# MLP of a decode-step layer: sums of the second projection's right factors stored beside the first projection's outputs, tiles over both token parts, and one sequence of products for both projections

## The chip, the core and the metric

One core of a Trainium2 chip runs the whole program. The engines named below are TensorE (PE; its weight loads are PEld), VectorE (DVE), ScalarE (ACT), GpSimd (POOL) and SyncE (SP), whose queue issues nearly all of the DMAs here. The metric is the device time of one execution in microseconds, the median of the runs shown.

## The reference

One layer of a hybrid network is computed for 1024 prompt tokens and 8 sample tokens of 1024 features, all in float32: three attention-like branches, their gated sum, an output projection, and an MLP. The change concerns the MLP alone:

```
x  = x + merged @ w_out
h2 = rmsnorm(x, norm_ffn)
x  = x + square(relu(h2 @ w_up)) @ w_down        # w_up 1024 x 4096, w_down 4096 x 1024
```

## The kernel before

Activations lie feature-major, 128 features on the partitions and 1032 tokens in a row. A float32 product is made of three: each factor is split into a high half, which the matrix engine takes exactly (a copy on ACT), and a low half (a subtraction on DVE, in the helper `low`, line 1310), and high x high, high x low and low x high are added up in PSUM.

From the output projection on, the tokens are taken in four quarters of 258 (`HQ`). Quarter l x part s: the part s (0 or 1) pairs two quarters, l (0 or 1) is the half of tokens in Strassen's scheme. Both projections of the MLP use Winograd's form of that scheme: 7 products P1 to P7 instead of 8, whose **left factors** are blocks of weights or sums of them (S1 to S4), and whose **right factors** are blocks of activations or sums of them (T1 = B12 - B11, T2 = B22 - T1, T3 = B22 - B12, T4 = B21 - T2). `CHAIN` says which PSUM bank a product adds into: P1, P6, P7 and P4 run up in one bank (two such banks), P5 and P3 in another, P2 in a third, and the partial sums are read on the way. So P6 has to wait until P1's sum was read, P7 for P6's, P4 for P7's, and P3 for P5's.

`stream` runs through units of seven products, in the order P1, P5, P4 of the unit before, P6, P2, P3, P7. It makes left factors ahead, as far as there are places for them (six in the first projection, four in the second): the sums on POOL (`add`, line 1460), the high half on ACT (line 1489), the low half on DVE. Weights are loaded two units ahead.

- **First projection** (`w_up`): 16 units of 256 hidden features; a product is 24 matmuls of 258 columns. `done_up` reads the sums out, applies the squared ReLU, and leaves four tiles `us` of 128 x 516 (128 features; l is fixed, both parts s), which SP stores in DRAM as `u`.
- **Second projection** (`w_down`): 24 units. The contraction over 4096 hidden features is cut into six parts of 2, 3, 3, 3, 3, 2 pairs of hidden blocks, and each part has four units j = 0 to 3 of 256 output features; a product is 12 or 18 matmuls. `done_dn` adds each of the seven products to the residual `x` (line 1636, DVE, 128 x 516).
- **Right factors of the second projection.** For each of the 16 pairs r, `feed` loads its four blocks from `u` into tiles `ub`, and makes T1, T2 and T3 on POOL (`sums`, lines 1326 to 1328), T4 later (lines 1588, 1645 or 1669). `factor` splits each of the seven, for each part s by itself: 14 copies on ACT (line 1320) and 14 subtractions on DVE, 128 x 258 each. The first two pairs are fed while the first projection runs; the others while the second one does. In a part, one or two pairs are fed ahead, the rest (`late`) during its last unit j = 3, when the part's own factors come free.

Code is written in this order, but instructions are put on the engines by a list scheduler that moves what it takes to be ready; each engine then works through its own list in order, and an instruction that waits holds up all behind it.

Of the kernel before, what the change touches and what calls it, by code (L numbers as in the profile page):

```python
# [89 lines left out]
def tile_step(ctx, tc, I, O):  # L90
# [98 lines left out]
    # activations in feature-major form, as pairs of exact halves, one tile for each group of tokens  # L189
# [64 lines left out]
    def in_proj(c0, evac):  # L254
        # a piece is split once the products two pieces before it have been taken out, not when it is thought to arrive
# [57 lines left out]
    # the loras' weights as exact halves: the high one over both halves of their inputs, the low one over the high  # L313
# [155 lines left out]
        # k, and for each head the sums that normalize kk and that weigh v beside the state; both go from a column per  # L469
        # head to all of its features by way of DRAM  # L470
# [52 lines left out]
        # scaled by the decay within each chunk  # L523
# [13 lines left out]
        # products within each chunk, and token-major forms  # L537
# [15 lines left out]
        # (the latter as they count at the end of their chunk)  # L553
# [15 lines left out]
        # inverse of the unit lower triangular matrices: first of their two diagonal blocks, each partition  # L569
        # with a quarter of the columns of one block  # L570
# [18 lines left out]
        # and the block beside them, two matrices in a product of which the diagonal blocks count  # L589
# [15 lines left out]
        # chunk after chunk, both pairs at once  # L605
# [41 lines left out]
        # group norm, then the sum and the gate  # L647
# [29 lines left out]
        # a sample's part of the window that stays  # L677
# [59 lines left out]
    # last token's projections  # L737
# [76 lines left out]
    def rwkv_sample():  # L814
        # one step of the sample group, a half of a head's values in each partition
# [64 lines left out]
    def xsample():  # L880
        # the sample group: scores by products along the features, since each sample has its own memory
# [124 lines left out]
    # keys  # L1006
# [24 lines left out]
    # values  # L1031
# [116 lines left out]
    def ssample():  # L1148
        # the sample group: each sample has its own past keys and values
# [87 lines left out]
    def split_out(pool, d, x=""):  # L1237
        # a branch's output, as a pair of exact halves
# [73 lines left out]
    def parts(t):  # L1312
        # a row of tokens in its four quarters
# [4 lines left out]
    def factor(key, s, i, x):  # L1318
        hi, lo = mk(cb[s], f"h{i}", [P, HQ], F32R, 4), mk(cb[s], f"l{i}", [P, HQ], F32R, 4)
        A.activation(hi, x, AF.Copy)  # L1320
        low(lo, x, hi)
        right[key, s, i] = hi, lo

    def sums(b11, b12, b21, b22, t1, t2, eng):
        # T1, T2 and T3; T3 takes the place of B12
# [363 lines left out]
    for r in pairs[0][2:]:  # L1689
        for _ in feeding(r):  # L1690
            pass
# [29 lines left out]
```

## Time and profile before

| | us |
|---|---|
| median of 3 runs | 2095.15 |
| fastest, slowest of the 3 | 2092.27, 2095.73 |
| the profiled execution, from its first to its last instruction (span) | 2090.5 |
| busy in it: PE, DVE, ACT, POOL | 1931.6, 1381.6, 765.4, 569.6 |
| first projection | about 1350 to 1698 |
| second projection | about 1698 to 2081 |

For the profiled execution only the span is given, no time of its own: it is 4.65 us under the median, and this distance is taken to be outside the program's instructions. A time worked out as a change of the span is therefore carried over to the median as it is. PE is busy for 92% of the span. In a program whose stages are all bound by the same engine the remaining 8% would be spread evenly; the table of stretches further down tells whether they are.

### The profile page before, as it was taken

The numbers are of one execution on the slowest core, as the hardware profiler recorded it, in microseconds if no ns is written. First come the engines' busy times: TensorE is split into PE (matmuls) and PEld (weight loads), VectorE is DVE, ScalarE is ACT, GpSimd is POOL, SyncE is SP. The second block draws the span as 40 slices with busy tenths as digits, with TensorE's granted clock in tenths as the row PEclk, the third lists the DMA queues.
The fourth block names the chain that finished last, engine by engine and source line by source line (L and its number), as shares of the span: only waits on it lengthen the run. The fifth ranks groups of instructions, "written<-read, shape, count | busy, mean of one in ns | idle before, by whom it ended". The sixth has DMA issues, their size and how long they took to land. (4 is left out here: it accounts for less than half of the span.)

```text
span 2090.5 us, 36979 instructions
## 1 busy us (share of the span) xinstructions
PE 1931.6 (92%) x14079; PEld 1832.6 (88%) x14079; DVE 1381.6 (66%) x3359; ACT 765.4 (37%) x1729; POOL 569.6 (27%) x606
## 2 busy tenths in 40 slices
PE   4989889999999989999899999889999988998898
PEld 4879878888888978998799999879999988998897
DVE  7455767576765375676723674885545599888974
ACT  5432333232323244345641132443333353433433
POOL 3422111110110244231110000364222246456531
PEclk9999989798989999999899999989999999999999
DMA  4543223323221154232253446334333353222213
GB/s 140 167 161 117 87 73 93 83 85 91 82 78 36 58 187 133 52 116 71 81 168 123 154 131 209 97 96 128 117 97 107 107 198 102 88 83 90 78 45 102
DMA packets 243278, 225.31 MB, mean 108 GB/s; under 512 B 41565, under 2 KB 203422, under 8 KB 243102
## 3 DMA queue, kind: packets, MB, share of 16 engines
q1 hardware_dynamic: 240832, 215.88, 33.5%
q0 software_dynamic: 2016, 6.53, 1.0%
q8 instruction: 111, 1.82, 0.4%
q10 hardware_dynamic: 254, 0.55, 0.1%
q14 instruction: 65, 0.53, 0.1%
HBM read 161.51 MB, written 61.78 MB: 107 GB/s over the span
## 5 line engine op out<-in xcount | busy, mean ns | idle before, releaser
L181 PE MATMUL mm<-hh,wh 128*128 128x384 f32 (+1 forms) x1152 | 391.6, 340 | 5.4 <-ACT z L342 4.8
L182 PE MATMUL mm<-hl,wh 128*128 128x384 f32 (+1 forms) x1152 | 388.9, 338 | 7.3 <-DVE hl L217 7.3
L183 PE MATMUL mm<-hh,wl 128*128 128x384 f32 (+1 forms) x1152 | 388.4, 337 | 1.3 <-POOL wl L174 1.3
L1506 PE MATMUL z<-h,wh 128*128 128x258 f32 x1504 | 269.6, 287 | 22.4 <-DVE x L1636 9.0
L1506 PE MATMUL z<-h,wl 128*128 128x258 f32 x1488 | 265.3, 287 | 22.8 <-DVE x L1636 21.5
L1506 PEld LDWEIGHTS z<-h,wh 128*128 128x128 f32 x1504 | 220.8, 193 | 26.8 <-issue 6.0
L1506 PEld LDWEIGHTS z<-h,wl 128*128 128x128 f32 x1488 | 217.1, 192 | 25.9 <-issue 18.3
L182 PEld LDWEIGHTS mm<-hl,wh 128*128 128x128 f32 x1152 | 227.0, 197 | 11.3 <-DVE hl L217 8.2
L181 PEld LDWEIGHTS mm<-hh,wh 128*128 128x128 f32 x1152 | 227.4, 197 | 9.5 <-ACT z L342 5.2
L183 PEld LDWEIGHTS mm<-hh,wl 128*128 128x128 f32 x1152 | 227.3, 197 | 5.0 <-POOL wl L174 1.7
L174 POOL TENSOR_TENSOR wl<-wst,wh 128x1024 fp32r<-128x1024 f32 x48 | 116.8, 2434 | 213.6 <-ACT wh L173 210.1
L1506 PE MATMUL z<-l,wl 128*128 128x258 f32 x744 | 153.9, 287 | 3.1 <-DVE l L1310 3.1
L1506 PE MATMUL z<-l,wh 128*128 128x258 f32 x752 | 155.8, 287 | 1.0 <-DVE l L1310 1.0
L1636 DVE TENSOR_TENSOR x<-z,x 128x516 f32<-128x516 f32 x168 | 115.4, 687 | 56.3 <-PE z L1506 56.3
L173 ACT ACTIVATE wh<-wst 128x1024 fp32r<-128x1024 f32 x84 | 88.8, 1057 | 138.6 <-PE mm L182 74.1
L1310 DVE TENSOR_TENSOR l<-ub,h 128x258 fp32r<-128x258 f32 x224 | 124.0, 602 | 1.4 <-ACT h L1320 1.3
L1506 PEld LDWEIGHTS z<-l,wh 128*128 128x128 f32 x752 | 119.7, 194 | 1.7 <-DVE l L1310 1.7
L1506 PEld LDWEIGHTS z<-l,wl 128*128 128x128 f32 x744 | 117.8, 192 | 3.7 <-DVE l L1310 3.6
L1320 ACT ACTIVATE h<-ub 128x258 fp32r<-128x258 f32 x224 | 78.6, 409 | 67.3 <-POOL ub L1645 31.4
L183 PE MATMUL mm<-oh,wl 128*128 128x384 f32 (+1 forms) x288 | 92.2, 320 | 0.0
L182 PE MATMUL mm<-ol,wh 128*128 128x384 f32 (+1 forms) x288 | 92.1, 320 | 0.0
L181 PE MATMUL mm<-oh,wh 128*128 128x384 f32 (+1 forms) x288 | 92.0, 319 | 0.0
(518 smaller groups left out, 4247.5 us busy)
## 6 DMA issues: line engine op xcount, KB each, us to landing
wst<-in_w_in SPq DMA_DIRECT2D x48, 512.0 KB
u<-us SPq DMA_DIRECT2D x64, 258.0 KB
ub<-u SPq DMA_DIRECT2D x64, 258.0 KB
wst<-in_w_down SPq DMA_DIRECT2D x24, 512.0 KB
gate<-gt SPq DMA_DIRECT2D x48, 192.0 KB
gl<-gate SPq DMA_DIRECT2D x16, 516.0 KB
wst<-in_w_out SPq DMA_DIRECT2D x16, 512.0 KB
wst<-in_w_up SPq DMA_DIRECT2D x16, 512.0 KB
```

Of the source, the lines that this page charges most:

```text
L173: A.activation(hi, st, AF.Copy)
L174: last_lo[:] = [eng.tensor_tensor(lo, st, hi.bitcast(F32), ALU.subtract)]
L181: PE.matmul(out, lhsT=wh, rhs=xh, start=first and k == 0, stop=False)
L182: PE.matmul(out, lhsT=wh, rhs=xl, start=False, stop=False)
L183: end = PE.matmul(out, lhsT=wl, rhs=xh, start=False, stop=last and k == n - 1)
L1310: V.tensor_tensor(lo, x, hi.bitcast(F32), ALU.subtract)
L1320: A.activation(hi, x, AF.Copy)
L1506: op = PE.matmul(z[:, s, :HQ], lhsT=t[:, a, k], rhs=right[ks[k], s, i][b], start=go and k + q == 0, stop=q == 2 and k == nk - 1, skip_grou ...
L1636: V.tensor_tensor(c, z, c, ALU.add)
```

## The change

1. `done_up` makes T1, T2, T3 and T4 itself, on POOL, from the tiles `us` that are still in SBUF (`diff`, line 1607 of the new kernel), and stores seven tiles for each unit instead of four. `u` gets the shape [16, 7, 128, 2, 258]: one contiguous tile for each right factor. `us` has 6 buffers instead of 3, `cv` 4 instead of 5.
2. `feed` loads one of the seven right factors at a time; POOL has nothing to do for it.
3. `factor_u` splits a right factor over both parts s at once: one copy on ACT and one subtraction on DVE, 128 x 516 each, into tiles of [128, 2, 258]. Pair r takes a place in pool `cb[r % 2]`.
4. Both projections run in one `stream` of 40 units, so that the first products of the second projection come ahead of P4 of unit 15, and its weights are loaded like any other unit's. The left factors of the second projection take only the places of `ring`.

```diff
-    u_d = mk(dr, "u", [32, P, NT])
+    u_d = mk(dr, "u", [16, 7, P, 2, HQ])
...
-    def factor(key, s, i, x):
-        hi, lo = mk(cb[s], f"h{i}", [P, HQ], F32R, 4), mk(cb[s], f"l{i}", [P, HQ], F32R, 4)
+    def factor_tiles(c, i):
+        return [mk(cb[c], f"{x}{i}", [P, 2, HQ], F32R, 2) for x in "hl"]
+
+    def factor(k, s, i, x):
+        if (k // 2, s, i) not in twos:
+            twos[k // 2, s, i] = factor_tiles(s, i)
+        hi, lo = [t[:, k % 2] for t in twos[k // 2, s, i]]
         A.activation(hi, x, AF.Copy)
         low(lo, x, hi)
...
+    def factor_u(r, i, x):
+        hi, lo = factor_tiles(r % 2, i)
+        A.activation(hi, x, AF.Copy)
+        low(lo, x, hi)
+        for s in range(2):
+            right[("u", r), s, i] = hi[:, s], lo[:, s]
...
             while at[0] < len(seq) and seq[at[0]][0] in raw:
                 u, i = seq[at[0]]
+                ok = [sl for sl in free if u < NU or sl[0] is ring]
+                if not ok:
+                    return
...
-        if ss.stop == 2:
-            SY.dma_start(parts(u_d[2 * u + a])[:, l], us[u, i])
-
-    def feed(r, early=False):
-        b = []
-        for j in range(2):
-            for l in range(2):
-                b.append(ubt())
-                SY.dma_start(b[-1], parts(u_d[2 * r + j])[:, l])
-        t1, t2 = [mk(tf[1], "tf", [P, 2, HQ], F32, 4) if early else ubt() for _ in range(2)]
-        feeds[r] = sums(*b, t1, t2, G)
+        def put(k, t):
+            SY.dma_start(u_d[u, k - 1], t)
+
+        def diff(k, x, y, t=None):
+            t = mk(up, "us", [P, 2, HQ], F32, 6) if t is None else t
+            G.tensor_tensor(t, x, y, ALU.subtract)
+            tq[u, k] = t
+            put(k, t)
+
+        if i == 2:
+            put(1, o)
+        if i in (2, 3) and {(u, 2), (u, 3)} <= whole:
+            diff(5, us[u, 3], us[u, 2])
+        if {(u, 7), (u, 3), (u, 2)} <= whole and (u, 6) not in tq:
+            put(3, us[u, 7])
+            diff(6, us[u, 7], tq[u, 5])
+            diff(7, us[u, 7], us[u, 3], us[u, 3])
+        if i == 4:
+            put(2, o)
+            diff(4, o, tq[u, 6])
+
+    def feed(r, i):
+        feeds[r, i] = ubt()
+        SY.dma_start(feeds[r, i], u_d[r, i - 1])
+
+    def feed_put(r, i):
+        factor_u(r, i, feeds.pop((r, i)))
...
-    for r in pairs[0][2:]:
-        for _ in feeding(r):
-            pass
-    stream(4 * len(SZ), load_dn, lambda t, a, j: t.rearrange("p (r j) (i n) -> p r j i n", j=2, i=2)[:, :, j, a],
-           lambda u: [("u", r) for r in pairs[u // 4]], done_dn, rs + rs, after=after)
+    rs = [(ring, "wh", 2), (ring, "wl", 2)]
+    stream(NU + 4 * len(SZ), done, rs + [(pb, "pa", 1)] + rs + [(pb, "pb", 1)], lead, after)
```

What this does to the lists of the engines is shown at two places. The first is **POOL in the middle of the first projection**. Before, its list has nothing but the four sums `sw` of each unit's left factors (`wst`, `wsx` are raw weights):

```order
L1460 TENSOR_TENSOR sw_2418_16373<-wst_2402_16186 128x512
L1460 TENSOR_TENSOR sw_2419_16375<-sw_2418_16373,wst_2401_16185 128x512
L1460 TENSOR_TENSOR sw_2420_16377<-wst_2401_16185,sw_2419_16375 128x512
L1460 TENSOR_TENSOR sw_2435_16536<-wst_2401_16185,wst_2402_16186 128x512
L1460 TENSOR_TENSOR sw_2441_16599<-wsx_2425_16412 128x512
```

After, the four differences of a unit's outputs `us` stand between them:

```order
L1503 TENSOR_TENSOR sw_2311_15699<-wsx_2292_15502 128x512
L1607 TENSOR_TENSOR us_2297_15564<-us_2296_15561,us_2294_15530 128x516
L1503 TENSOR_TENSOR sw_2312_15701<-sw_2311_15699,wsx_2291_15501 128x512
L1607 TENSOR_TENSOR us_2300_15598<-us_2299_15594,us_2297_15564 128x516
L1607 TENSOR_TENSOR us_2296_15561<-us_2299_15594,us_2296_15561 128x516
L1503 TENSOR_TENSOR sw_2313_15703<-wsx_2291_15501,sw_2312_15701 128x512
L1607 TENSOR_TENSOR us_2310_15696<-us_2309_15692,us_2300_15598 128x516
L1503 TENSOR_TENSOR sw_2330_15869<-wsx_2291_15501,wsx_2292_15502 128x512
```

So POOL has eight instructions for each unit of the first projection where it had four, and the second, third and fourth sum of a unit's left factors stand behind differences that wait for products of an earlier unit.

The second place is **DVE where a part of the second projection ends** and the late right factors are split: `x` <- `z` is the addition to the residual that frees a PSUM bank, `wl` and `wh` are low halves of left factors, `l` those of right factors. Before:

```order
L1636 TENSOR_TENSOR x_2728_18386<-z_2902_19385,x_2728_18386 128x516
L1310 TENSOR_TENSOR wl_19761<-sw_19758,wl_19761 128x384
L1310 TENSOR_TENSOR l_2993_19777<-ub_19209,h_2992_19776 128x258
L1310 TENSOR_TENSOR l_2995_19781<-ub_19222,h_2994_19780 128x258
L1310 TENSOR_TENSOR l_2997_19785<-ub_19222,h_2996_19784 128x258
L1636 TENSOR_TENSOR x_2628_18008<-z_2966_19662,x_2628_18008 128x516
L1310 TENSOR_TENSOR wh_19807<-wst_19604,wh_19807 128x256
L1310 TENSOR_TENSOR wh_19807<-wx_19606,wh_19807 128x128
L1310 TENSOR_TENSOR l_3000_19813<-ub_19691,h_2999_19812 128x258
L1310 TENSOR_TENSOR l_3002_19817<-ub_19691,h_3001_19816 128x258
L1310 TENSOR_TENSOR l_3009_19853<-ub_19693,h_3008_19852 128x258
L1636 TENSOR_TENSOR x_2628_18008<-z_3003_19820,x_2628_18008 128x516
```

After, at the same place:

```order
L1648 TENSOR_TENSOR x_2674_18391<-z_2815_19317,x_2674_18391 128x516
L1310 TENSOR_TENSOR wl_19642<-sw_19639,wl_19642 128x384
L1310 TENSOR_TENSOR l_2880_19654<-ub_19385,h_2879_19653 128x516
L1310 TENSOR_TENSOR l_2883_19682<-ub_19581,h_2882_19681 128x516
L1648 TENSOR_TENSOR x_2593_18031<-z_2858_19550,x_2593_18031 128x516
L1310 TENSOR_TENSOR wh_19676<-wst_19508,wh_19676 128x256
L1310 TENSOR_TENSOR wh_19676<-wx_19510,wh_19676 128x128
L1310 TENSOR_TENSOR l_2890_19718<-ub_19583,h_2889_19717 128x516
L1310 TENSOR_TENSOR l_2895_19750<-ub_19585,h_2894_19749 128x516
L1648 TENSOR_TENSOR x_2593_18031<-z_2884_19685,x_2593_18031 128x516
L1310 TENSOR_TENSOR wl_19714<-sw_19705,wl_19714 128x384
```

Between two additions there are now two subtractions of 516 columns instead of three of 258; the order of the kinds is the same.

## Rows read from the trace of the kernel before

**Rows 1.** The page: the span and the number of instructions.

```profile
span 2090.5 us, 36979 instructions
```

**Rows 2.** Stretches: length, busy PE, PEld, DVE, ACT, POOL, clock, DMA share, GB/s.

```profile
1390.00:1440.00 50.00, 50.00 (x419) 50.00 (x418) 40.55 (x38) 18.43 (x32) 32.72 (x21) 1.00 0.52 164
1440.00:1690.00 250.00, 250.00 (x2085) 250.00 (x2085) 132.28 (x191) 86.29 (x161) 69.53 (x52) 1.00 0.34 109
1690.00:1750.00 60.00, 47.65 (x367) 46.10 (x366) 58.75 (x105) 28.47 (x82) 31.82 (x31) 0.94 0.51 172
1750.00:1820.00 70.00, 64.60 (x513) 63.17 (x511) 62.89 (x109) 26.33 (x74) 39.04 (x46) 0.98 0.26 84
1820.00:1890.00 70.00, 61.80 (x505) 60.79 (x506) 62.53 (x111) 28.55 (x82) 40.19 (x45) 1.00 0.29 92
1890.00:1960.00 70.00, 63.76 (x504) 62.67 (x503) 60.21 (x110) 28.58 (x82) 40.75 (x45) 0.98 0.29 92
1960.00:2000.00 40.00, 34.02 (x263) 33.34 (x264) 35.00 (x64) 13.25 (x38) 19.26 (x24) 0.96 0.25 80
2000.00:2060.00 60.00, 59.54 (x495) 58.91 (x494) 41.88 (x83) 20.91 (x50) 14.66 (x21) 1.00 0.17 51
```

**Rows 3.** Waits of PE from 1380 us: releaser, total us, times, longest.

```profile
PE z L1506 <- DVE x L1636: 30.5, 23, 2.8
PE z L1506 <- DVE cv L1558: 6.4, 2, 5.3
```

**Rows 4.** Timeline of PE: start, us, instruction, count, idle before and releaser.

```profile
1697.89 0.80 PE L1506 MATMUL z<-h,wh 128*128 128x258 f32 x2 [5.28 <-DVE cv L1558]
...
1730.43 0.48 PE L1506 MATMUL z<-h,wl 128*128 128x258 f32 x2 [2.81 <-DVE x L1636]
```

**Rows 5.** Timeline of DVE in the same place and shortly before.

```profile
1722.27 0.75 DVE L1310 TENSOR_TENSOR l<-ub,h 128x258 fp32r<-128x258 f32 x2
...
1726.75 2.93 DVE L1310 TENSOR_TENSOR l<-ub,h 128x258 fp32r<-128x258 f32 x2
1729.60 0.68 DVE L1636 TENSOR_TENSOR x<-z,x 128x516 f32<-128x516 f32 x1
```

**Rows 6.** Timeline of POOL at 1726 us.

```profile
1726.50 1.47 POOL L1327 TENSOR_TENSOR ub<-ub,ub 128x516 f32<-128x516 f32 x1
1727.94 1.45 POOL L1328 TENSOR_TENSOR ub<-ub,ub 128x516 f32<-128x516 f32 x1
```

**Rows 7.** Stretches, instructions on tile ub alone: length, DVE, ACT, POOL, clock, DMA share, GB/s.

```profile
1690.00:1750.00 60.00, 24.90 (x46) 18.10 (x52) 18.17 (x13) 0.94 0.51 172
...
1820.00:1890.00 70.00, 23.19 (x42) 14.43 (x42) 18.57 (x13) 1.00 0.29 92
```

**Rows 8.** Groups by shape on DVE, 1820 to 1890 us: count, busy us, mean ns, idle.

```profile
L1310 DVE TENSOR_TENSOR l<-ub,h 128x258 fp32r<-128x258 f32 x42 | 23.2, 604 | 0.0
...
L1310 DVE TENSOR_TENSOR wl<-sw,wl 128x384 fp32r<-128x384 f32 x8 | 6.3, 784 | 0.0
...
L1310 DVE TENSOR_TENSOR wh<-wst,wh 128x256 fp32r<-128x256 f32 x6 | 3.8, 629 | 0.0
```

**Rows 9.** Stretch of the same 70 us, line 1310 on DVE alone.

```profile
1820.00:1890.00 70.00, 47.00 (x83) 1.00 0.29 92
```

**Rows 10.** Groups by shape on DVE, 2000 to 2060 us.

```profile
L1310 DVE TENSOR_TENSOR wh<-wst,wh 128x256 fp32r<-128x256 f32 x6 | 2.8, 461 | 0.0
L1310 DVE TENSOR_TENSOR wl<-sw,wl 128x384 fp32r<-128x384 f32 x4 | 2.2, 554 | 0.0
```

**Rows 11.** Groups by shape, 1440 to 1660 us.

```profile
L1555 DVE TENSOR_TENSOR us<-us 128x516 f32<-128x516 f32 x10 | 7.0, 696 | 16.7 <-ACT us L1554 16.7
```

**Rows 12.** The page: DMA issues, count and KB of each.

```profile
u<-us SPq DMA_DIRECT2D x64, 258.0 KB
```

**Rows 13.** Timeline of DVE in the first projection.

```profile
1517.13 0.69 DVE L1310 TENSOR_TENSOR wl<-wst,wl 128x512 fp32r<-128x512 f32 x1 [2.18 <-ACT wl L1489]
```

**Rows 14.** Timeline of PE in the first projection, the first matmul on that tile.

```profile
1530.19 0.41 PE L1506 MATMUL z<-h,wl 128*128 128x258 f32 x2
```

More of the change, by code (lines that the diff above doesn't have):

```diff
@@ L1432, in tile_step @@
     cnt_u, feeds = [0], {}
+    NU = 16
+    SZ = (2, 3, 3, 3, 3, 2)
+    pairs = [range(sum(SZ[:c]), sum(SZ[:c + 1])) for c in range(len(SZ))]
+    ORDER = (1, 5, 6, 2, 3, 7, 4)
     def ubt(shape=(P, 2, HQ)):
@@ L1436, in ubt, with load, block, keys @@
         return mk(ub[cnt_u[0] % len(ub)], "ub", shape, F32, 4)
-    def stream(units, load, block, keys, done, slots, lead=None, after=None):
+    def load(u):
+        if u < NU:
+            t = [mk(*((wsx[1], "wsx") if u % 2 else (ring, "wst")), [P, KT, P], F32, 2) for _ in range(2)]
+            for i in range(2):
+                SY.dma_start(t[i], wup[:, :, (2 * u + i) * P:(2 * u + i + 1) * P])
+            return [t]
+        u -= NU
+        r, c = pairs[u // 4], u % 4 * 256
+        t = [mk(ring, "wst", [P, 4, 256], F32, 2)]
+        SY.dma_start(t[0], wdn[:, 2 * r[0]:2 * r[0] + 4, c:c + 256])
+        if len(r) == 3:
+            t.append(mk(dp[1], "wx", [P, 2, 256], F32, 2))
+            SY.dma_start(t[1], wdn[:, 2 * r[2]:2 * r[2] + 2, c:c + 256])
+        return t
+    def block(u, t, a, j):
+        if u < NU:
+            return t[a][:, 4 * j:4 * j + 4]
+        return t.rearrange("p (r j) (i n) -> p r j i n", j=2, i=2)[:, :, j, a]
+    def keys(u):
+        return range(4) if u < NU else [("u", r) for r in pairs[(u - NU) // 4]]
+    def stream(units, done, slots, lead, after):
         seq = []
         for u in range(units + 1):
-            for i in (1, 5, 4, 6, 2, 3, 7) if u or not lead else (1, 5, 6, 3, 7, 2):
+            for i in (1, 5, 4, 6, 2, 3, 7) if u else (1, 5, 6, 3, 7, 2):
                 if i == 4 and u > 0:
@@ L1448, in stream @@
         raw, ws, left, zt = {0: load(0)}, {}, {}, {}
-        if not lead:
-            raw[1] = load(1)
         at = [0]
@@ L1474, in fill @@
         def fill():
-            while at[0] < len(seq) and seq[at[0]][0] in raw and free:
+            while at[0] < len(seq) and seq[at[0]][0] in raw:
                 u, i = seq[at[0]]
+                ok = [sl for sl in free if u < NU or sl[0] is ring]
+                if not ok:
+                    return
                 at[0] += 1
@@ L1491, in fill @@
                 left[u, i] = t, sl
-                if i == 4 and u + 2 < units:
-                    raw[u + 2] = load(u + 2)
+                if i == 4:
+                    split.add(u)
+                    if u + 2 < units:
+                        raw[u + 2] = load(u + 2)
         def prod(u, i, ss):
@@ L1515, in stream @@
         fill()
-        n = 0
-        if lead:
-            for n, (u, i) in enumerate(seq[:6]):
-                with tc.issue_after(prod(u, i, (0,)).ins):
-                    lead(n)
-            raw[1] = load(1)
-            for u, i in seq[:6]:
-                prod(u, i, (1,))
-                release(u, i)
-            n = 6
-        while n < len(seq):
-            u, i = seq[n]
+        for n, (u, i) in enumerate(seq[:6]):
+            with tc.issue_after(prod(u, i, (0,)).ins):
+                lead(n)
+        raw[1] = load(1)
+        for u, i in seq[:6]:
+            prod(u, i, (1,))
+            release(u, i)
+        for u, i in seq[6:]:
             prod(u, i, (0, 1))
             release(u, i)
-            if after:
-                after(u, i)
-            n += 1
-    cv, us = {}, {}
-    wsx, tf = [], []
-    def load_up(u):
-        t = [mk(*((wsx[1], "wsx") if u % 2 else (ring, "wst")), [P, KT, P], F32, 2) for _ in range(2)]
-        for i in range(2):
-            SY.dma_start(t[i], wup[:, :, (2 * u + i) * P:(2 * u + i + 1) * P])
-        return [t]
+            after(u, i)
+    cv, us, tq, split, whole = {}, {}, {}, set(), set()
+    wsx, tf, dp, x1 = [], [], [], []
     def done_up(u, i, z, ss):
@@ L1573, in feed_put @@
[L1573 to L1588 removed]
+        if ss.stop < 2:
+            return
@@ new lines, in done_up, with load_x1 @@
+        if i == 4:
+            put(2, o)
[5 more added lines that the diff above has]
+        factor_u(r, i, feeds.pop((r, i)))
+    def load_x1(n):
+        if not x1:
+            wsx[0].close()
+            dp.append(sbuf("down0")[1])
+        if len(x1) == 2:
+            for st in (tf[0], up_, pb_):
+                st.close()
+            ub.remove(tf[1])
+            dp.append(sbuf("down1", "right")[1])
+            ub.append(sbuf("ub3", "right")[1])
+        for m in range(len(x1), len(x1) + n):
+            x1.append(mk(dp[-1], f"x{m}", [P, NT]))
+            SY.dma_start(x1[m], x1_d[m])
@@ L1590, in tile_step, with done_dn, done @@
+    def done_dn(u, i, z, ss):
+        a, l = {1: (0, 0), 2: (0, 0), 5: (1, 1), 7: (1, 1), 6: (0, 1), 3: (0, 1), 4: (1, 0)}[i]
+        c = parts(x1[2 * (u % 4) + a])[:, l]
+        V.tensor_tensor(c, z, c, ALU.add)
+    def done(u, i, z, ss):
+        done_up(u, i, z, ss) if u < NU else done_dn(u - NU, i, z, ss)
     norm = second_norm(1)
@@ L1638, in tile_step, with late, late_put @@
-    fq = []
-    def feeding(r):
-        feed(r)
-        f = feeds[r]
-        for i in (1, 5, 6, 2, 3, 7, 4):
+            ub.append(tf[1])
+    fq, due = [], []
+    def feeding(r):
+        for i in ORDER:
+            feed(r, i)
+        for i in ORDER:
+            feed_put(r, i)
+            yield True
+    def late(rs):
+        todo = [(r, i) for i in ORDER for r in rs]
+        for f in todo[:PLACES]:
+            feed(*f)
+        due[:] = todo[PLACES:]
+    def late_put(rs, i):
+        for r in rs:
+            feed_put(r, i)
+        for _ in rs:
+            if due:
+                feed(*due.pop(0))
@@ L1644, in feeding, with after_up @@
+    PLACES = 11
+    def after_up(u, i):
+        if u == 13 and i == 4:
+            late(range(2))
+        if u == 15:
+            if i == 7:
+                assert 15 in split
+                load_x1(2)
+            late_put(range(2), i)
             if i == 4:
-                G.tensor_tensor(f[4], f[2], f[6], ALU.subtract)
-            feed_put(r)(i, f[i])
-            yield True
+                load_x1(2)
     def after(u, i):
+        if u < NU:
+            return after_up(u, i)
+        u -= NU
@@ L1655, in after @@
             ahead = [r for r in pairs[c + 1] if r - 4 < pairs[c][0]]
-            late = [r for r in pairs[c + 1] if r not in ahead]
+            rest = [r for r in pairs[c + 1] if r not in ahead]
             if j < len(ahead) and i == 1:
```

72 lines of the change are left out of this document (12 added, 60 removed).

## The prediction

> **What bounds the kernel now.** The page gives the span [rows 1], and the waits of PE say for whom it stood still: 30.5 us for the residual additions `x` and 6.4 us for two copies `cv` [rows 3], both on DVE. To see where, I read the table by stretches [rows 2]. In the 250 us of the first projection PE is busy without a gap at clock 1.00 and gets 2085 matmuls done, 250 / 2085 = 0.120 us each; that is the price of a matmul when nothing holds it up. What a stretch loses is its length less its matmuls at this price:
>
> - 1690 to 1750: 60 - 367 x 0.12 = 16.0 us
> - 1750 to 1820: 70 - 513 x 0.12 = 8.4; 1820 to 1890: 9.4; 1890 to 1960: 9.5
> - 1960 to 2000: 40 - 263 x 0.12 = 8.4
> - 2000 to 2060: 60 - 495 x 0.12 = 0.6
>
> Together about 52 us, nearly all while right factors are being made. In the three 70 us stretches DVE is busy for 60 to 63 of 70, in the first one for 58.75 of 60; in the last part, where no right factors are left to load, it is busy for 42 of 60, and PE loses nothing. So the second projection is set by DVE, and PE waits for its additions. (The part of the loss that isn't in the waits is PE working at a clock of 0.94 to 0.98 after gaps, in the same table.)
>
> Why DVE is so full is seen in its timeline. Two subtractions of a right factor take 0.75 us when undisturbed; at 1726.75 the same two take 2.93 us [rows 5], and just then POOL runs two sums of right factors, 1726.50 to 1729.39 [rows 6]. The addition behind them starts at 1729.60, and PE, which needs its bank, has been idle for 2.81 us when it goes on at 1730.43 [rows 4]. A subtraction from SBUF and a POOL sum do not run side by side here.
>
> **Sums that leave the second projection.** POOL spends 18.57 us of the 70 us stretch at 1820 on tiles `ub`, 13 instructions of 1.4 us, and 18.17 us of the stretch at 1690 [rows 7]. They go, and POOL falls from 40.2 [rows 2] to 21.6 us there, 0.31 of the time. How fast DVE's subtractions are then is bounded by the last part, where POOL is busy for 14.66 of 60 us, 0.24: a 128 x 384 subtraction takes 554 ns there and a 128 x 256 one 461 [rows 10], against 784 and 629 at 1820 [rows 8], ratios of 0.71 and 0.73. With 0.31 instead of 0.24 I take 0.8. The left factors' share of line 1310 is 47.0 [rows 9] - 23.2 = 23.8 us and falls by 4.8. The bounds: nothing, and 0.72, which is 6.7.
>
> **Subtractions over both parts.** 42 of 258 columns become 21 of 516. Undisturbed, two took 0.75 [rows 5] and one of 516 columns between two SBUF tiles takes 0.696 [rows 11], so the merging itself saves 0.05 us each, 1 us per stretch. Disturbed, a pair costs 23.2 / 21 = 1.10 now, 0.35 of it from POOL; by POOL's share 0.19 of that remains. One of 516 is then about 0.70 + 0.19 = 0.89 us, 21 of them 18.7: 4.5 us less.
> The Trainium skill, Perfetto Trace Analysis, section Optimizing Scalar/DVE Operations, puts DVE's overhead at about 60 ns for an instruction on SBUF; by it the 112 instructions that go would be worth an estimated 6.7 us in all, the rows give 5.6.
>
> **Sum for a full stretch.** DVE at 1820: 62.5 - 4.8 - 4.5 = 53.2 us, against 505 x 0.12 = 60.6 that PE needs. PE then sets the pace. At a part's end DVE still has, between two additions, one left factor and two right ones: 0.69 + 0.5 + 2 x 0.7 = 2.6 us against a product of 18 x 0.12 = 2.16, so I leave 2 us of loss in each part. Gains: 8.4 - 2 = 6.4, 7.4, 7.5, 6.4. In the stretch at 1690 PE needs only 44.0, since products of 12 matmuls and 46 subtractions of right factors fall together: DVE 58.75 - 4.4 (23 pairs) - 3.2 (15.8 us of left factors x 0.2) = 51.2, so 7.2 of the 16.0 remain, gain 8.8. Sum 36.5 us.
>
> **The seam** is in that 8.8. PE waits 5.28 us at 1697.89 for DVE's `cv` [rows 4]: P4 of unit 15 has only 8 matmuls of other work ahead of it. Now P1 and P5 of unit 16 stand there, 24 matmuls, 2.9 us against 1.0, which covers about 2 us.
>
> **The first projection** gets the sums: four differences per unit, 5.6 us, on top of POOL's 69.5 us in 250. A unit is 168 x 0.12 = 20.1 us long, so POOL has 5.6 + 5.6 = 11.2 of 20.1, and DVE, at 132 of 250 us, 10.6 before any new contention. If each difference held up one DVE subtraction for its whole time, DVE would be at 16.2 of 20.1. The cover is long: a bank is needed again two products of 24 matmuls later, 5.8 us. And the stretch at 1390 has POOL at 32.7 of 50 and DVE at 40.6, and PE still 50.00 busy [rows 2]. So I price the contention at nothing for PE; without the cover it would be up to 5.6 us a unit. POOL's left sums now stand behind differences that wait for products. A low half done at 1517.82 [rows 13] is first used by PE at 1530.19 [rows 14], 12.4 us of slack; a difference in front of each of three sums costs 4.2, and nothing falls due.
> DMA: 48 more stores and 48 more loads of 258 KB, to 64 stores before [rows 12] and, four blocks a pair, 64 loads, at a DMA share of 0.34 in the first projection and 0.26 to 0.29 in the second. SP's queue holds the weight loads behind the stores, and a store waits for its difference; the weights are loaded two units ahead, 40 us. At the seam the loads come just in time, so I take 2 us off, between 0 and the 5.6 us of a unit's four differences.
>
> **Sum:** 36.5 - 2 = about 35 us. The profiled span goes from 2090.5 to 2055.5, and with its distance of 4.65 to the median the forecast is 2060. Its own range is 2046 (all 52 us but 3 come back) to 2069 (a loss of 4 us in each of the five stretches instead of 2).
>
> **Rivals.**
>
> *R1, the contention only moves.* The differences meet DVE's `cv` and `us` chain in the first projection, where the sums now take POOL past half of the time, and PE, gapless today, waits. For it: rows 5 and 6 are about the instructions themselves, not about the stage. Against it: the stretch at 1390. Were one of the four differences' worth of delay to reach PE with two thirds of its 1.4 us, it would be 1 us for each of 16 units: 2060 + 16 = 2076.
> The Trainium skill says, on the same page and section, that GpSimd and VectorE share an SBUF read port, so that handing work from one to the other may not help. The trace agrees with the sharing (2.93 against 0.75 us), and it is the reason for R1; that PE would feel it in the first projection, no row shows.
>
> *R2, DVE still sets the second projection.* A longer subtraction in front of an addition makes the addition later: 0.70 us where half of a pair, 0.375, may have stood before. With 0.32 us for each of the 25 waits of [rows 3] that is 8 us, and if the factor of 0.8 isn't reached either, 20 to 30 us of the 52 stay lost instead of 15: 2065 to 2075, and with the 8 us on top of the middle some 2078. I take 2075.
> The same section of the Trainium skill says that where VectorE is not saturated and still causes bubbles, instructions should be broken up, the reverse of this edit; today VectorE is saturated here (62.5 of 70), after it may not be, and then the rule would speak.
>
> *R3, slower.* POOL works in order, and the differences in front of the second, third and fourth left sum wait for products of an earlier unit and for a free tile `us`, which waits for a store. When such a wait exceeds the slack of 12.4 us, every unit of the first projection is late. It decides at 35 / 16 = 2.2 us a unit beyond the slack; at 4 us it is 64 - 35 = 29 us slower, 2124. Against it: three sums and three differences are 8.4 us of work within 12.4.
>
> *R4, no change.* The seven loads for a pair, where there were four, come late at a part's end: 35 us over 14 pairs is 2.5 us a pair. Against it: the DMA share of 0.29, and PE names no load among its waits; for it, the pool of tiles `ub` keeps its 4 buffers, and a pair now takes seven of them in turn. 2095.
>
> **How the numbers follow.** Forecast 0.65, R1 0.12, R2 0.13, R3 0.05, R4 0.05. A difference of 0.2%, 4 us, is about what a measurement of this kernel can tell from none. Faster: 0.65 + 0.12 + 0.13 = 0.90, the same 0.05, slower 0.05. The range goes from 2046 to 2084, R2 and R1 with 8 us above them; outside are R3, R4 and the tails of the others, less than 0.2.
>
> **What would show it.** Right: between 1440 and 1690 PE is busy without a gap, with POOL near 139 of 250 and DVE above 132; from 1750 on a 70 us stretch holds some 565 matmuls instead of 505, POOL about 22 us in it and DVE below 57; a right factor's subtraction of 516 columns averages under 0.95 us; PE's waits for `x` fall from 30.5 to about 10 us, and the one of 5.28 at the seam to about 3. R1 would show as waits of PE for `cv` or for `wl`, `wh` in the first projection, R2 as DVE above 58 of 70, R3 as PE waiting for left factors behind a long wait of POOL, R4 as DVE and ACT waiting for `ub`. I am wrong in the main step if the subtractions stay at 0.75 of their present time or above with POOL's sums gone, for then it isn't POOL that slows them.

## The result, and the profile after

The changed kernel takes 2062.39 us (median of 4 runs, 2058.34 to 2067.74) against 2095.44 us before in the same rounds: a ratio of 0.9845 with a 95% interval of 0.9804 to 0.9887. The forecast was 2060, the range 2046 to 2084. One execution in this study, of the kernel with 75 extra subtractions below, was slow (2112.39 us, at a granted clock of 0.935), and its median leaves it out.

The page of the profiled execution begins:

```profile
span 2061.0 us, 36994 instructions
```

The stretches of [rows 2] in the changed kernel (length, busy PE, PEld, DVE, ACT, POOL, clock, DMA share, GB/s):

```profile
1390.00:1440.00 50.00, 46.44 (x369) 45.85 (x368) 37.16 (x45) 17.54 (x32) 34.12 (x24) 0.96 0.62 191
1440.00:1690.00 250.00, 250.00 (x2083) 250.00 (x2082) 156.24 (x175) 81.59 (x141) 144.95 (x102) 1.00 0.45 149
1690.00:1750.00 60.00, 53.86 (x427) 52.90 (x426) 52.82 (x87) 28.52 (x60) 24.23 (x23) 0.97 0.85 278
1750.00:1820.00 70.00, 70.00 (x584) 70.00 (x583) 58.26 (x107) 33.77 (x77) 28.58 (x37) 1.00 0.49 144
1820.00:1890.00 70.00, 70.00 (x581) 69.97 (x580) 57.97 (x105) 30.59 (x69) 32.57 (x38) 1.00 0.53 153
1890.00:1960.00 70.00, 69.94 (x580) 69.75 (x579) 55.75 (x104) 29.48 (x66) 31.36 (x39) 1.00 0.43 129
```

From 1750 us on PE is busy all but without a gap, with 580 to 584 matmuls in 70 us where there were 504 to 513. In the 250 us of the first projection POOL has gone from 69.5 to 145 us and DVE from 132 to 156, and PE did as many matmuls as before (2083 against 2085). In the stretch at 1390 PE is now busy for 46.4 us instead of 50, and DMA is busy for 0.85 of the stretch at 1690. The waits of PE from 1380 us on (releaser, total us, times, longest), which answer to [rows 3]:

```profile
PE z L1555 <- DVE x L1648: 4.5, 3, 2.7
...
PE z L1555 <- DVE cv L1594: 2.9, 3, 1.3
```

They were 30.5 and 6.4 us. Groups by shape in the stretch at 1820, for [rows 8], first DVE, then POOL:

```profile
L1310 DVE TENSOR_TENSOR l<-ub,h 128x516 fp32r<-128x516 f32 x28 | 20.9, 773 | 0.5 <-ACT h L1335 0.5
L1310 DVE TENSOR_TENSOR wl<-sw,wl 128x384 fp32r<-128x384 f32 x10 | 6.2, 625 | 0.0
...
L1310 DVE TENSOR_TENSOR wh<-wst,wh 128x256 fp32r<-128x256 f32 x7 | 2.9, 414 | 0.0
```

```profile
L1503 POOL TENSOR_TENSOR sw<-wx 128x128 f32<-128x128 f32 x9 | 9.6, 1070 | 0.0
L1503 POOL TENSOR_TENSOR sw<-wst 128x256 f32<-128x256 f32 x9 | 8.2, 912 | 34.1 <-DMA wst<-in_w_down 21.8 <-DVE wl L1310 6.3 <-DVE wh L1310 5.9
```

A subtraction of 384 columns fell from 784 to 625 ns, one of 256 from 629 to 414. POOL's sum of 128 columns, however, took 544 ns before:

```profile
L1460 POOL TENSOR_TENSOR sw<-wx 128x128 f32<-128x128 f32 x8 | 4.3, 544 | 0.8 <-DMA wx<-in_w_down 0.7
```

**Where the time went, in sections.** The spans of two executions differ ahead of the MLP too, where the engines' lists are the same: in the 13 traces of this study the MLP's first matmul starts between 1341.7 and 1365.9 us. So I cut the MLP at events that each kernel has: its first matmul; the 42nd addition `cv` on DVE (in unit 12 of the first projection); the 28th addition to `x` (end of the first of six parts); the 168th (the last). The differences to the kernel before, from the timelines of PE and DVE, are below; the last column is their sum.

| kernel | first projection | its end and first part | other five parts | sum |
|---|---|---|---|---|
| before (us long) | 285.8 | 124.4 | 325.2 | 735.4 |
| after | +4.3 | -9.2 | -31.7 | -36.6 |
| after, once more | +4.6 | -7.7 | -32.4 | -35.5 |
| extra POOL subtractions, 59 | +3.5 | -2.1 | -11.8 | -10.4 |
| extra POOL subtractions, 75 | +4.8 | -2.1 | -6.9 | -4.2 |
| extra POOL fills | +4.3 | -6.5 | -32.0 | -34.2 |
| sums at the load | +0.2 | -2.4 | +2.5 | +0.3 |
| sums at the load, 258 columns | +2.2 | -0.4 | +4.9 | +6.7 |
| after with 258 columns | +4.6 | -8.3 | -32.3 | -36.0 |
| differences doubled | +27.6 | +6.8 | -32.5 | +1.9 |
| P4 first at the seam | +6.5 | -8.0 | -32.1 | -33.6 |
| unit 0's differences later | +0.2 | -4.7 | -31.5 | -36.0 |
| the same, and feeds later | +0.5 | -8.5 | -33.9 | -41.9 |

Each line is one execution. The two of the changed kernel differ by 1.1 us in the sum and 1.5 in one section; differences of 2 us are not told from none here.

### The profile page after: what moved, and what is told of

Its sections match the earlier page's. It is cut to its first block, busy times and chain, and to the rows that moved or that the text cites. A ratio compares the mean times of both kernels' runs of the same rounds, so it can differ in the third digit from the quotient of the medians.

```text
span 2061.0 us, 36994 instructions
## 1 busy us (share of the span) xinstructions
PE 1928.9 (94%) x14079; PEld 1834.5 (89%) x14079; DVE 1344.0 (65%) x3247; ACT 755.8 (37%) x1617; POOL 590.7 (29%) x606
## 3 DMA queue, kind: packets, MB, share of 16 engines
q1 hardware_dynamic: 254656, 241.24, 38.5%
## 5 line engine op out<-in xcount | busy, mean ns | idle before, releaser
L1555 PE MATMUL z<-h,wh 128*128 128x258 f32 x1488 | 263.2, 285 | 8.1 <-DVE wh L1310 4.9
L1555 PEld LDWEIGHTS z<-h,wh 128*128 128x128 f32 x1488 | 216.1, 192 | 9.2 <-DVE wh L1310 5.1
L1503 POOL TENSOR_TENSOR sw<-wst 128x256 f32<-128x256 f32 (+1 forms) x56 | 55.1, 984 | 208.0 <-DMA wst<-in_w_down 87.9
L1607 POOL TENSOR_TENSOR us<-us,us 128x516 f32<-128x516 f32 x64 | 96.5, 1519 | 52.0 <-issue 22.1
L1310 DVE TENSOR_TENSOR l<-ub,h 128x516 fp32r<-128x516 f32 (+1 forms) x120 | 92.9, 800 | 6.3 <-ACT h L1335 6.1
```

The lines of the kernel that those rows point to most:

```text
L1310: V.tensor_tensor(lo, x, hi.bitcast(F32), ALU.subtract)
L1503: G.tensor_tensor(s[:, k:k + n], v, w, op)
L1555: op = PE.matmul(z[:, s, :HQ], lhsT=t[:, a, k], rhs=right[ks[k], s, i][b], start=go and k + q == 0, stop=q == 2 and k == nk - 1, skip_grou ...
L1607: G.tensor_tensor(t, x, y, ALU.subtract)
```

## Experiments

**The changed kernel again** (no edit).

> The changed kernel once more, in rounds with the kernel before: 2058 to 2066 us, 30 to 36 us under the kernel before. In the profile of the change PE had lost 8.6 us more than before by 1330 us, in code that the change leaves alone. If that is the spread between executions, this profile puts that stretch elsewhere within some us and the same stretch from 1390 us on at the same length; if the change causes it, it comes again.

2061.43 us against 2094.8, ratio 0.9838 (0.9805 to 0.9872). Its MLP starts at 1352.2 us, 6 us after that of the kernel before, as in the first profile of the change; but other kernels with the same lists up to there start at 1341.7 or 1365.9. So the late start is taken as the spread of executions, although it came again, which was to be the sign of the change.

**Extra subtractions on POOL in the second projection**, which nobody reads:

```diff
         SY.dma_start(feeds[r, i], u_d[r, i - 1])
+        if r > 1 and i in (5, 6, 7, 4):
+            extra(feeds[r, i], 2 if i == 4 and r % 2 else 1)
...
+        for _ in range(n):
+            G.tensor_tensor(idle[0], x[:, :, :224], x[:, :, :224], ALU.subtract)
```

> The changed kernel, and beside each right factor 5, 6, 7 and 4 that the second projection loads a subtraction on POOL that nobody reads (128 x 448, on the loaded tile; 59 in all, some 51 of 516 columns' worth). Theory, the gain is POOL's work gone from DVE's side: DVE's subtractions slow down again and most of the gain of the second projection goes, 2082 to 2092 us. Rival, the gain is that the sums were a step between a load and its split: nothing waits for these, so 2062 to 2067 us.

2088.47 us, ratio 0.996 (0.9932 to 0.9988): 27 us more than the changed kernel in the same rounds. The stretch at 1820 and two groups from 1690 to 2020 us:

```profile
1820.00:1890.00 70.00, 67.06 (x536) 66.19 (x535) 60.40 (x94) 29.97 (x67) 40.88 (x49) 0.98 0.46 133
```

```profile
L1631 POOL TENSOR_TENSOR ex<-ub 128x448 f32<-128x448 f32 x59 | 63.8, 1082 | 16.6 <-DMA ub<-u 14.5
...
L1310 DVE TENSOR_TENSOR l<-ub,h 128x516 fp32r<-128x516 f32 x106 | 100.0, 967 | 4.5 <-ACT h L1335 4.4
```

POOL is busy for 40.9 of 70 us, as before the change, and PE does 536 matmuls instead of 581. A right factor's subtraction takes 967 ns, against 790 in the changed kernel from 1690 to 2000 us (the row stands with the fills). Nobody waits for these results, so what costs here is POOL's work itself, by its reading or by its being busy; the fills below tell the two apart. DVE's additions `x`, which read one factor from PSUM, are not slowed: 688 ns here, 690 in the changed kernel and 686 before, over the same time.

```profile
L1660 DVE TENSOR_TENSOR x<-z,x 128x516 f32<-128x516 f32 x136 | 93.5, 688 | 44.0 <-PE z L1555 43.8
```

**The same with 75 of them:**

```diff
-            extra(feeds[r, i], 2 if i == 4 and r % 2 else 1)
+            extra(feeds[r, i], 2 if i == 4 or i == 7 and r > 5 else 1)
```

> As the run with extra subtractions on POOL in the second projection, with some 75 of them instead of 59, which makes POOL's added time about that of the sums at the load (82 us). Theory, POOL's time beside DVE is all of the loss: what the second projection takes more grows with it, from 27 us to 34 us or more, 2094 to 2102 us. Rival, the rest between the 27 us and the 41 us of the sums at the load is the step from load to sum to split: no more than before, 2086 to 2091 us.

2089.98 us (median of 11 executions), ratio 0.9961 (0.9925 to 0.9998): inside the rival's range, and by time not to be told from the 59, since both intervals are over 10 us wide. In the sections it loses 4.9 us more than the 59 in the five parts, so the loss seems to grow with POOL's time, by one execution of each. But it takes 82.3 us on POOL for these (1690 to 2030 us), as many as the sums at the load do (81.8, below), and still is 9 us better than those over the second and third sections (-9.0 against +0.1).

```profile
L1631 POOL TENSOR_TENSOR ex<-ub 128x448 f32<-128x448 f32 x75 | 82.3, 1097 | 12.8 <-DMA ub<-u 9.4
```

So POOL's time beside DVE is most of the loss, and not all of it.

**Fills instead of subtractions**, with no less time on POOL:

```diff
-            G.tensor_tensor(idle[0], x[:, :, :224], x[:, :, :224], ALU.subtract)
+            G.tensor_tensor(idle[0][:, 0, :1], x[:, 0, :1], x[:, 0, :1], ALU.subtract)
+            for _ in range(2):
+                G.memset(idle[0], 0.0)
```

> As the run with extra subtractions on POOL in the second projection, but each of them replaced by a subtraction of one column and two fills of 128 x 448 with zero, which read nothing. Theory, it is POOL's reading that stops DVE's subtractions from SBUF: the fills cost little, 2061 to 2068 us. Rival, any POOL instruction in SBUF slows DVE, by its duration: 2078 to 2092 us.

2057.13 us, 4 under what was expected at least, ratio 0.9802 (0.9752 to 0.9851), like the changed kernel. The stretch at 1820, and the groups from 1690 to 2000 us:

```profile
1820.00:1890.00 70.00, 69.83 (x577) 69.65 (x577) 58.09 (x107) 29.59 (x67) 46.40 (x88) 1.00 0.53 155
```

```profile
L1633 POOL MEMSET ex<- 128x448 f32 x118 | 55.8, 473 | 6.3
...
L1310 DVE TENSOR_TENSOR l<-ub,h 128x516 fp32r<-128x516 f32 x105 | 78.3, 767 | 3.7 <-ACT h L1335 3.6
```

In the changed kernel, same stretch:

```profile
L1310 DVE TENSOR_TENSOR l<-ub,h 128x516 fp32r<-128x516 f32 x109 | 83.6, 790 | 5.9 <-ACT h L1335 5.8
```

POOL is busier here (46.4 of 70) than it was before the change, and DVE's subtractions do not notice it: 767 ns against 790. The one-column subtractions read the same loaded tiles as the 448 columns did, and left sums stand behind the fills as they did behind the subtractions, so a tile held longer or a sum made later is not what cost the 27 us. Instruction by instruction, the 22 subtractions of this trace that no POOL instruction with a factor in SBUF overlaps (three of them beside a fill) take 680 to 698 ns, and the 83 that one overlaps up to 1242. It is POOL's reading from SBUF that stops a subtraction with both factors in SBUF, not its being busy. The Trainium skill, Perfetto Trace Analysis, section Optimizing Scalar/DVE Operations, speaks of an SBUF read port that GpSimd and VectorE share; the trace agrees, 967 ns beside reads against 767 beside fills.

**The sums at the load, in the second projection**, all else as in the change (four stores a unit, seven loads a pair):

```diff
-        if i == 2:
-            put(1, o)
...
+        SY.dma_start(u_d[u, {2: 1, 3: 7, 7: 3, 4: 2}[i] - 1], o)
...
+        t = feeds[r, i] = ubt()
+        SY.dma_start(t, u_d[r, {5: 7, 6: 3, 4: 2}.get(i, i) - 1])
+        if i in (5, 6, 7, 4):
...
+            G.tensor_tensor(t, x, y, ALU.subtract)
```

> The changed kernel with the sums of the right factors back in the second projection, on POOL at the load (seven loads a pair as in the change, four stores a unit as before, both parts split at once, one sequence). Theory, the place of the sums is the gain: 2082 to 2095 us, PE in the stretch of the middle parts 5 to 9 us short of 70 again. Rival, merging, the one sequence and the new order of loads make the gain: 2060 to 2068 us.

2102.28 us, ratio 1.0028 (0.9998 to 1.0057): 41 us more than the changed kernel, 7 over what was expected at most, and not faster than the kernel before. From 1820 us, and DVE, POOL and ACT on right factors from 1690 to 2020 us:

```profile
1820.00:1890.00 70.00, 62.15 (x487) 61.44 (x486) 58.24 (x88) 27.17 (x61) 38.84 (x43) 0.95 0.42 123
```

```profile
L1310 DVE TENSOR_TENSOR l<-ub,h 128x516 fp32r<-128x516 f32 x101 | 102.3, 1036 | 4.8 <-ACT h L1335 4.3
...
L1610 POOL TENSOR_TENSOR ub<-ub,ub 128x516 f32<-128x516 f32 x57 | 81.8, 1441 | 29.1 <-DMA ub<-u 17.3 <-DVE l L1310 9.7 <-DVE x L1632 1.4
L1335 ACT ACTIVATE h<-ub 128x516 fp32r<-128x516 f32 x101 | 59.9, 627 | 38.6 <-POOL ub L1610 26.9 <-DMA ub<-u 6.8 <-PE z L1555 3.4
```

So with the sums in their old place the merged split, the one sequence and the new loads together are worth nothing (the sections give +0.3 us); the place of the sums decides.

**258 columns instead of 516**, once in the changed kernel and once with the sums at the load:

```diff
-        A.activation(hi, x, AF.Copy)
-        low(lo, x, hi)
         for s in range(2):
+            A.activation(hi[:, s], x[:, s], AF.Copy)
+            low(lo[:, s], x[:, s], hi[:, s])
```

> The changed kernel with each right factor split for each token part by itself: 224 pairs of 258 columns instead of 112 of 516. Theory, merging is a small term (0.05 us for each of the instructions saved): 5 to 8 us more than the change, 2067 to 2070 us. Rival, short instructions let the additions come sooner: no more than the change, 2055 to 2062 us. Rival, merging is the main cause: 2080 us or more.

> The kernel with the sums at the load, and each right factor split for each token part by itself. Here DVE sets the second projection, so that the merging should show: by the prediction's term, 4.5 us for each 70 us stretch, 14 to 18 us more than with 516 columns, 2116 to 2120 us. Rival: the two halves of a split let the additions come sooner and the merging is worth nothing even here, 2098 to 2106 us.

2062.96 us in the changed kernel (ratio 0.985, 0.9808 to 0.9891), between the ranges expected, and no difference to 516 columns in time (2061.43) or sections (-36.0 against -36.6 and -35.5). With the sums at the load 2105.51 (ratio 1.0036, 0.9999 to 1.0074; in other rounds than its partner), a ratio 0.0008 over that of 516 columns, inside both intervals, and as the rival expected; in the sections it is 2.4 us longer in the five parts and 6.4 in all, of which 2.0 lie in the first projection, where nothing differs. From 1690 to 2030 us its subtractions take:

```profile
L1310 DVE TENSOR_TENSOR l<-ub,h 128x258 fp32r<-128x258 f32 x210 | 121.9, 630 | 1.1 <-ACT h L1336 1.1
```

That is 121.9 / 105 = 1.16 us busy for a pair, against 102.3 / 101 = 1.01 for one of 516: 0.15 us of DVE each. Where DVE sets the pace, merging saves DVE time (some 16 us for 105 pairs), of which at most some 4 us reach PE; where PE sets it, it saves nothing that can be read.

**The differences doubled in the first projection** (the same values written again, eight instructions a unit for four):

```diff
-            G.tensor_tensor(t, x, y, ALU.subtract)
+            for _ in range({5: 3, 7: 1}.get(k, 2) if u else 1):
+                G.tensor_tensor(t, x, y, ALU.subtract)
```

> The changed kernel with eight differences on POOL for each unit of the first projection (from unit 1 on) instead of four; the same values are written again. POOL gets some 5.6 us more per unit, 17 of 20.1. Theory, the matmuls of the first projection cover what DVE loses: PE stays gapless from 1440 to 1690 us, 2060 to 2066 us. Rival, the cover is just enough for one set (R1 of the prediction, only later): 1 us or more for each of 15 units, 2076 us or more.

2100.59 us, ratio 1.0019 (0.9991 to 1.0048): the whole gain is gone. The long stretch of the first projection, and two waits in it:

```profile
1440.00:1690.00 250.00, 238.14 (x1946) 234.50 (x1945) 156.97 (x160) 71.75 (x127) 196.86 (x135) 1.00 0.44 140
```

```profile
DVE us L1595 <- POOL us L1608: 24.5, 10, 2.5
PE z L1555 <- DVE cv L1594: 11.9, 19, 1.4
```

POOL is busy for 197 of 250 us, and DVE waits for tiles `us` that POOL still holds, with the next `cv` behind, for which PE waits. With one set of differences POOL has 145 of 250 and no engine of this chain waits for it. The cover that the prediction counted on is there for four differences a unit, and not for eight. What gives way is POOL itself, which gives the tiles back late, and not DVE's busy time, which stays at 157 us; PE's waits for `cv` are the sign that the prediction gave for R1.

**P4 of unit 15 first**, with nothing between it and P7 in the order of the code:

```diff
-            for i in (1, 5, 4, 6, 2, 3, 7) if u else (1, 5, 6, 3, 7, 2):
+            for i in (4, 1, 5, 6, 2, 3, 7) if u == NU else (1, 5, 4, 6, 2, 3, 7) if u else (1, 5, 6, 3, 7, 2):
```

> The changed kernel with P4 of unit 15 ahead of P1 and P5 of unit 16, so that nothing stands between P7 and P4. Theory of the prediction, the 24 matmuls cover DVE's reading: without them 3 us or more are lost, 2065 to 2068 us. Rival, DVE sets the stretch around the seam anyway (8.6 us are lost there before and after the change): within 1.5 us, 2060 to 2064 us.

2060.21 us, ratio 0.9843 (0.9793 to 0.9893); the section that holds the seam is at -8.0 us, between the two of the change. So the order of P4 is worth nothing there. But the cover works: the longest wait for `cv` at the seam is, in the changed kernel and in this run,

```profile
1708.00 0.48 PE L1555 MATMUL z<-h,pb 128*128 128x258 f32 x2 [1.14 <-DVE cv L1594]
```

```profile
1724.37 0.80 PE L1555 MATMUL z<-h,wh 128*128 128x258 f32 x2 [5.56 <-DVE cv L1594]
```

With 8 matmuls ahead of it, as before the change, P4 waits 5.56 us again, where it had waited 5.28. What follows makes up for most of it: PE waits 1.6 us for `x` from 1690 to 1760 us, where the changed kernel waits 4.5.

**Unit 0's differences behind unit 1's left sums** (`made[1, 3]` is the third of them):

```diff
-            G.tensor_tensor(t, x, y, ALU.subtract)
+            with tc.issue_after(made[1, 3].ins) if u == 0 else ExitStack():
+                G.tensor_tensor(t, x, y, ALU.subtract)
```

> The changed kernel with the differences of unit 0 put behind the first three left sums of unit 1 on POOL. Theory: where the first projection starts, POOL waits 3.7 us for unit 0's outputs with those sums behind it, and that is why the 500 matmuls from 1330 us on take 3 to 4 us longer than before; they lose it again, PE's wait of 1.8 us for wl goes, 2057 to 2060 us. Rival: the sums are late for another reason (their weights), no difference, 2060 to 2064 us.

2062.91 us, ratio 0.9834 (0.9794 to 0.9875), no difference in time, as the rival expected. The first projection's section, however, is at +0.2 us instead of +4.3 and +4.6. POOL at that place in the changed kernel, and what PE waits for:

```profile
1397.57 4.30 POOL L1607 TENSOR_TENSOR us<-us,us 128x516 f32<-128x516 f32 x3 [3.73 <-DVE us L1595]
1401.83 1.26 POOL L1503 TENSOR_TENSOR sw<-wsx 128x512 f32<-128x512 f32 x1
```

```profile
1403.81 0.50 PE L1555 MATMUL z<-h,wl 128*128 128x258 f32 x2 [1.77 <-ACT wl L1536]
```

And POOL with the edit:

```profile
1403.97 1.28 POOL L1503 TENSOR_TENSOR sw<-wsx 128x512 f32<-128x512 f32 x1 [3.53 <-DMA wsx<-in_w_up]
...
1408.62 1.75 POOL L1608 TENSOR_TENSOR us<-us,us 128x516 f32<-128x516 f32 x1
```

The three left sums now come first, PE's wait for `wl` is gone, and the 4 us with it; the sums now wait 3.53 us for their weights. The next section is at -4.7 instead of -9.2 and -7.7 in this execution: what the start gave was lost again there, and this run does not show by what.

**The same, and pairs 2 and 3 fed one unit later:**

```diff
-            if j < len(ahead) and i == 1:
-                fq.append(feeding(ahead[j]))
+            if 0 <= j - (c == 0) < len(ahead) and i == 1:
+                fq.append(feeding(ahead[j - (c == 0)]))
```

> The kernel with unit 0's differences behind unit 1's left sums, and the pairs 2 and 3 fed during the units j = 1 and 2 of the first part instead of j = 0 and 1. Theory: around the seam DMA is what is late (21 loads of right factors, 11 stores and 6 loads of x in 50 us; ACT waits for loaded factors, DVE's additions for x and behind the subtractions), so that seven loads and seven subtractions fewer there give back some 5 of the 9 to 13 us lost there, and the lead 3 to 4: 2050 to 2056 us. Rival: DVE's own work there (cv, us and the first additions) sets the seam, and nothing changes but the lead: 2057 to 2063 us.

2060.29 us against 2100.45 in its rounds, ratio 0.9819 (0.9767 to 0.987), 4 us over the theory's range and inside the rival's. By time it cannot be told from the changed kernel (0.9838, 0.9805 to 0.9872); by its sections it is 5 to 6 us shorter over the MLP (-41.9), 4 of them at the start. What holds PE up longest at the seam of the changed kernel is read there:

```profile
1709.05 0.64 ACT L1335 ACTIVATE h<-ub 128x516 fp32r<-128x516 f32 x1 [3.17 <-DMA ub<-u]
...
1712.69 2.94 ACT L1335 ACTIVATE h<-ub 128x516 fp32r<-128x516 f32 x5 [1.17 <-DMA ub<-u]
```

```profile
1712.63 4.22 DVE L1310 TENSOR_TENSOR l<-ub,h 128x516 fp32r<-128x516 f32 x5
...
1717.38 0.68 DVE L1648 TENSOR_TENSOR x<-z,x 128x516 f32<-128x516 f32 x1
```

```profile
1718.21 0.50 PE L1555 MATMUL z<-h,wl 128*128 128x258 f32 x2 [2.70 <-DVE x L1648]
```

ACT waits for loaded right factors, then five come at once, their five subtractions hold DVE for 4.2 us, and the addition that PE waits for stands behind them. That the later feeds cured part of this is argued from one execution, whose second section (-8.5) lies between the two of the change; only against the run before (-4.7) is it better.

## Why the prediction came out right

- **POOL's sums slow DVE, and that sets the second projection:** shown. Put back beside DVE as work that nobody reads, they take 26 to 27 us of some 40 back with 59 instructions and 31 to 32 with 75 (second and third sections together: -13.9 and -9.0 against -40.9 and -40.1). Fills take 2 us (-38.5), which is not told from none. Left open are the last 9 us up to the kernel with the sums at the load; the step from load to sum to split is the likely cause, for in that kernel ACT waits 26.9 us for those sums before its copies `h`, and ACT's `wl` holds PE up:

```profile
PE z L1555 <- ACT wl L1536: 8.8, 5, 2.4
```

  With 75 extra subtractions that wait is 2.8 us (from 1690 us on, as this one). The step was not tried by itself.
- **Sizes in the stretch at 1820.** The left factors' 0.8 was right for 384 columns (625 / 784) and too careful for 256 (414 / 629 = 0.66). A right factor's subtraction takes 0.77 us, where 0.89 was worked out. POOL did not fall to 21.6 but to 32.6 us: there are 38 left sums in the stretch instead of 32, since PE is faster, and each is longer (912 ns instead of 834 for 256 columns). DVE is busy 58.0 us where 53.2 was worked out, but with 581 matmuls in place of the 505 that the sum counted; for 505 it would be 58.0 x 505 / 581 = 50.4. Two of the prediction's own signs would therefore mislead: DVE is above the 58 that was to show R2 (58.26 from 1750 us), and the 384 columns are above the 0.75 that was to show the main step wrong, a bound that the 0.8 of the sum is above as well. What decides is that PE has no gap, and the runs with extra work on POOL.
- **A loss of 2 us in each part:** too much. The stretches from 1750 on lose nothing that can be read (581 x 0.12 = 69.7). The other five parts gained 32 us, where the gains of the four stretches from 1750 on add up to 27.7.
- **Merging:** priced at 0.05 us of DVE's time for each instruction saved. Where DVE sets the pace a merged pair saves 0.15 us; in the changed kernel nothing of it reaches PE, for PE sets the pace there and DVE has 12 us of 70 to spare. The sum says so too, since its 70 us stretches end at what PE needs, and the term enters the forecast only by about 1 us in the stretch at 1690; POOL's part alone brings DVE under PE's need. R2's other side, that shorter instructions let additions come sooner, doesn't show either: 2062.96 against 2061.43. The Trainium skill's advice to break up instructions (same page and section as above) is for an engine that isn't saturated and yet causes bubbles on others; in the middle of the second projection there are none left, and it makes no difference in this kernel.
- **The seam:** the gain of 8.8 us at 1690 was about right in size (9.2 and 7.7 for the section). The 24 matmuls cover what they were to cover, for the stall of 5.28 us for `cv` falls to 1.14 and comes back without them (5.56). But the 2 us that this was to be worth are not there: with the stall or without it the section is as long, and in the changed kernel PE stands for `x` behind late loads instead. That step of the prediction failed, inside a sum that held.
- **The first projection:** its price of nothing for contention was right. The contention did move there, as R1 has it: a 512-column subtraction takes 1002 ns on average instead of 691, and POOL's differences 1512. From 1440 to 1690 us, first before, then in the changed kernel:

```profile
L1310 DVE TENSOR_TENSOR wl<-sw,wl 128x512 fp32r<-128x512 f32 x16 | 11.1, 691 | 8.2 <-ACT wl L1489 8.0
```

```profile
L1310 DVE TENSOR_TENSOR wl<-sw,wl 128x512 fp32r<-128x512 f32 x17 | 17.0, 1002 | 6.3 <-ACT wl L1536 6.0
...
L1607 POOL TENSOR_TENSOR us<-us,us 128x516 f32<-128x516 f32 x51 | 76.6, 1512 | 36.2 <-issue 22.1 <-DVE us L1595 13.4 <-POOL sw L1503 0.7
```

  PE doesn't feel it (busy for 250.00 of 250 us), with 24 matmuls a product to cover it; the run with the differences doubled shows that this cover has an end. The 2 us taken off were 4.3 to 4.6, and lay at its start: differences that wait for outputs, with left sums behind them on POOL. That is R3's mechanism at one place, where the slack of 12.4 us, read in the middle of the stage, isn't there: PE waits 1.77 us for `wl`.
- **The total:** 35 us were forecast, 33 measured by the medians, 36 by the sections of the MLP. That it comes so near is in part luck: the second projection gave 40 to 41 us by the sections where 36.5 were worked out, and the start took 4.3 to 4.6 where 2 were. Two small slips did no harm. A loss of 4 us in each of five stretches gives 2070, where the prediction has 2069. And the 4.65 us between span and median are not outside the program's instructions: in the profiled execution of the changed kernel the span is 2061.0 and the time 2062.78 us, 1.8 apart, so that the rest is the spread of executions; carried over to the median it cancels.

## What to carry to other kernels

When two engines whose reads hold each other up share a stage that one of them bounds, work of the other costs time there even if nobody waits for it (63.8 us of POOL's subtractions cost 27 us), and may cost nothing in a stage that a third engine bounds: the same 64 instructions cost some 40 us in one place and 4 in the other. How much cover the new place has is tested by doubling the work there; here it held one set and not two. And look at the ends of a stage for themselves, since slack read in its middle is not to be had at its start or its seam.

## What the runs showed of the hardware

- 59 POOL subtractions from SBUF make the mean of DVE's subtractions there longer by a quarter (967 against 767 ns for 516 columns), and POOL's fills, with no less time on POOL, do not. DVE's additions with one factor in PSUM take 686 to 690 ns in either case.
- The wait is mutual. In the changed kernel a left sum of 128 x 128 took 2.04 us on POOL, and ended 0.3 us after two subtractions on DVE that had begun beside it:

```profile
1820.94 2.04 POOL L1503 TENSOR_TENSOR sw<-wx 128x128 f32<-128x128 f32 x1
```

```profile
1821.36 1.30 DVE L1310 TENSOR_TENSOR l<-ub,h 128x516 fp32r<-128x516 f32 x2
```

  From 1690 to 2000 us the ten such sums that no subtraction of line 1310 overlaps take 456 to 469 ns, and the 22 that one overlaps 1056 on average.
- The same lists of instructions ahead of the MLP took between 1342 and 1366 us in 13 executions, while the section of the last five parts differed by 0.7 us between two executions of one kernel. Differences of some us are read from sections of the trace sooner than from medians.
